# A two-layer encoder trunk on one core: the first modulation staged by channel block, and one product of each `down` parted at column 264

## The chip, the cores and the metric

The kernel runs on one core of a Trainium2 chip. The metric is the device time of one execution in microseconds (us), as the median of several runs. The core has a matrix engine (TensorE; PE in the profile, with its weight loads as PEld), a vector engine (VectorE, DVE), a scalar engine (ScalarE, ACT), GpSimd (POOL), and SyncE (SP), which here only issues DMAs.

## The reference

One batch of 256 tokens with 1024 channels goes through two layers. Each layer has three sub-layers, each with a modulated RMSNorm ahead of it and a gated residual behind it. All shifts, scales and gates come from the condition `c` by a matrix of 1024 x 9216 per layer.

```python
c_act = silu(c)
h = x
for l in range(2):
    mod = c_act @ ada_w[l] + ada_b[l]
    sh1, sc1, g1, sh2, sc2, g2, sh3, sc3, g3 = split(mod, 9)
    n1 = rms_norm(h, norm_g[l, 0]) * (1 + sc1) + sh1
    h = h + 0.5 * g1 * swiglu(n1, ffn_wg[l, 0], ffn_wu[l, 0], ffn_wd[l, 0])
    n2 = rms_norm(h, norm_g[l, 1]) * (1 + sc2) + sh2
    h = h + g2 * token_mixing(n2, ...)      # two kinds of attention, merged by gates
    n3 = rms_norm(h, norm_g[l, 2]) * (1 + sc3) + sh3
    h = h + 0.5 * g3 * swiglu(n3, ffn_wg[l, 1], ffn_wu[l, 1], ffn_wd[l, 1])
return rms_norm(h, final_g)
# swiglu(x, wg, wu, wd) = (silu(x @ wg) * (x @ wu)) @ wd, with d_ff = 2816
```

## The kernel before, in words

**Products of float32 in three parts.** Every float32 operand `r` is held as a rounded part `hi` (type fp32r) and a rest `lo = r - hi`. A product is `hi.hi + lo.hi + hi.lo`, three products of TensorE with one sum in PSUM (`mm3`, lines 85 to 87). For the weights ScalarE makes `whi` (a cast, line 307) and VectorE `wlo` (a subtraction, line 308); for the activations they are `nh` and `nl`, and `hh` and `hl` within an FFN.

**The stream of weights.** All weights and the ada matrix come from HBM in units of 1 MB (128 partitions x 2048 columns) in one fixed order, the list `stream`. `load_next` issues the DMAs of the next unit on SP into one of four `raw` buffers; `pump(n)` takes `n` half units: a half of a weight unit goes through `whi` and `wlo` into two of 23 slots, a half of an ada unit through a reduction over the partition's 1024 columns (`ada_col`, line 240: shift and scale of one block of 128 channels) or a multiply-add (`ada_gate`, line 256). A `raw` buffer is filled again when both halves are taken, and a slot is free when the last product with it has ended (`done`).

**An FFN.** d_ff is cut into 11 slabs of 256. `gate_up_mm` makes one slab: 8 channel blocks x 2 halves x (gate, up) x 3 = 96 products of 256 columns (the tokens), weights stationary. `gate_up_act` makes `hT = silu(g) * u` as `hh` and `hl`. `down(idx)` adds slab idx into four PSUM banks (two token halves t x two column halves hf): 24 products of 512 columns, `hT` stationary and the weights moving. The loop makes gate/up of slab idx and then `down(idx - 1)`; the last three `down` stand apart in the boundary with the residual and the next norm. `gate_bcast` adds the gate's vector over the partitions by four products with a matrix of ones (`gb`, lines 281 and 282) and is called at idx 7.

**The start.** The first sub-layer has no sub-layer ahead to hide behind. `c` is spread over the partitions (`cb`), both token halves are normed with one power operation on POOL each, scaled, transposed on TensorE (`nt`) and copied to `xsT`. `first` then goes through the eight channel blocks in four pairs u: `mod_k(u)` reduces two units of ada (scale and shift of two blocks), makes `nh` on ScalarE (line 1164), `nf` and `nl` on VectorE (lines 1165, 1167); `go(sl, u)` runs the products of the pair for each of four slabs at once (line 1180), so that eight PSUM banks are filled together. The weights of those four slabs come in units named `side`. Then `down(0)` follows, and the three other slabs' `down`.

**What sets the order.** The program is written in this order; a scheduler of the framework places the instructions of each engine, and `follow`, `queue` and `behind` add order without a wait. Each engine takes its instructions strictly in order.

Of the kernel before, what the change touches and what calls it, by code (L numbers as in the profile page):

```python
# [19 lines left out]
P = 128  # L20
# [16 lines left out]
CAP0, CAP1, CAP2, CAP3 = 12, 12, 14, 14  # L37

# [3 lines left out]
def trunk(tc, a):  # L42
    nc = tc.nc
    with (
# [69 lines left out]
        for hf in range(2):  # L114
            x = slice(hf * 512, (hf + 1) * 512)
            bank = gen("cb")
            nc.tensor.matmul(bank, ones[0:1, :], crow[hf], start=True, stop=True)
            cact = nc.scalar.activation(cb[:, x], bank, AF.Silu)
# [44 lines left out]
        for l, s in SUBS:  # L163
            w = weights(l, s)
            ad = list(ada_in[(l, s)])
            if (l, s) == (0, 0):
                c = cols(0, 0)
# [32 lines left out]
        def load_next():  # L200
            if nload[0] < len(stream):
# [3 lines left out]
                if u[0] == "side":  # L205

                    _, j, pr = u
                    for i in range(2):
                        x = slice((j % 2) * 1024, (j % 2 + 1) * 1024)
                        nc.sync.dma_start(raw[:, i * 1024:(i + 1) * 1024], a["w_gu"][0, 0, 2 * pr + i, j // 2][:, x])  # L210
# [24 lines left out]
        def ada_col(u, r, i):  # L235
# [6 lines left out]
            if i == 1:  # L242
# [3 lines left out]
                else:  # L246
                    tmp = small("sc1", (P, 2))
                    nc.vector.tensor_tensor(tmp, col[:, k], abc[:, l, s, 1, k], op=ALU.add)
                    nc.vector.scalar_tensor_tensor(m["a"][:, k], tmp, 1.0, ngc[:, l, s, k], op0=ALU.add, op1=ALU.mult)

# [42 lines left out]
        halves = {}  # L293
        pos = [0, 0]

        def pump(n=1):
            while n > 0 and pos[0] < len(stream):
                u = stream[pos[0]]
                isw = u[0] not in ("col", "gate")
# [4 lines left out]
                if isw:  # L304
                    hi = slot("whi", (P, 1024), F32R, "w")
                    lo = slot("wlo", (P, 1024), F32R, "w")
                    queue("act", nc.scalar.copy(hi, r))  # L307
                    queue("dve", nc.vector.tensor_tensor(lo, r, hi.bitcast(F32), op=ALU.subtract))  # L308
                    if u[0] == "side":
                        _, j, pr = u  # L310
                        halves[("gu", 0, 0, 2 * pr + i, j // 2, j % 2)] = (hi, lo)
                    else:
                        halves[u + (i,)] = (hi, lo)
# [226 lines left out]
        def ffn(i, nT, norm1, first, nT_next):  # L540
# [6 lines left out]
            def down_mm(idx, t, hf, last, y=slice(0, 512)):  # L547
# [602 lines left out]
        def first(nT, hT, down):  # L1150
# [4 lines left out]
            def mod_k(u):  # L1155
                pump(4)

                pump(1)
                m = mods[(0, 0)]
                nf = b2("nf", (P, 2, S))  # L1160
                for i in range(2):
                    k = 2 * u + i
                    src = xsT[k // 4][:, k % 4, :]
                    nc.scalar.activation(nh[:, k, :], src, AF.Identity, bias=m["sh"][:, k:k + 1], scale=m["a"][:, k:k + 1])
                    nc.vector.tensor_scalar(nf[:, i, :], src, m["a"][:, k:k + 1], m["sh"][:, k:k + 1], op0=ALU.mult, op1=ALU.add)
                kk = slice(2 * u, 2 * u + 2)
                behind["dve"] = nc.vector.tensor_tensor(nl[:, kk, :], nf, nh[:, kk, :].bitcast(F32), op=ALU.subtract)

            def go(sl, u):
                g, ub = banks[sl]  # L1170
                un, i = ("gu", 0, 0, sl, u // 2), u % 2
                wh, wl = half(un, i)

                for x, y in ((0, 0), (1, 0), (0, 1)):
# [10 lines left out]
            for u in range(4):  # L1185
                mod_k(u)
                if u % 2 == 1:
                    free(1)
# [119 lines left out]
```

## Time and profile before

| | |
|---|---|
| median of 3 runs | 1107.83 us (1107.62 to 1108.61) |
| profiled execution, device time | 1109.12 us |
| its span, first to last instruction | 1107.3 us |
| TensorE busy | 1089.7 us, 98% of the span, 7758 products |
| VectorE busy | 865.4 us, 78% |
| ScalarE busy | 588.7 us, 53% |
| POOL busy | 44.2 us, 4% |
| moved by DMA | 271.12 MB, mean 245 GB/s |

How to read it: the profile is one execution, some 1.8 us longer than the span of its instructions. "Busy" of TensorE runs from a product's start to its modelled end, so consecutive products overlap in it, and a busy TensorE can still take its products at different paces: the pace is the distance between the starts of two products. In a row of the timeline the first number is the start in us from the span's beginning, the second the duration in us.

### The profile page before, as it was taken

The numbers are of one execution on the slowest core, as the hardware profiler recorded it, in microseconds if no ns is written. First come the engines' busy times: TensorE is split into PE (matmuls) and PEld (weight loads), VectorE is DVE, ScalarE is ACT, GpSimd is POOL, SyncE is SP. The second block draws the span as 40 slices with busy tenths as digits, with TensorE's granted clock in tenths as the row PEclk, the third lists the DMA queues.
The fourth block names the chain that finished last, engine by engine and source line by source line (L and its number), as shares of the span: only waits on it lengthen the run. The fifth ranks groups of instructions, "written<-read, shape, count | busy, mean of one in ns | idle before, by whom it ended". The sixth has DMA issues, their size and how long they took to land.

```text
span 1107.3 us, 19106 instructions
## 1 busy us (share of the span) xinstructions
PE 1089.7 (98%) x7758; PEld 1008.1 (91%) x7758; DVE 865.4 (78%) x1378; ACT 588.7 (53%) x910; POOL 44.2 (4%) x52
## 2 busy tenths in 40 slices
PE   6999999999999999999999999999999999999997
PEld 5989999898999899999989999989889988999996
DVE  6997986899978798886589886469988779765543
ACT  5454473558664653535365445445776547544432
POOL 1000000230010000000000000004000000000000
PEclk9999999999999999999999999999999999999999
DMA  8998996379745298897449977553865455866501
GB/s 326 395 343 319 355 345 226 116 263 320 263 178 191 97 374 342 333 357 288 148 152 362 356 284 270 194 177 117 297 233 190 156 188 193 315 252 229 198 12 39
DMA packets 42585, 271.12 MB, mean 245 GB/s; under 512 B 5624, under 2 KB 6392, under 8 KB 12544
## 3 DMA queue, kind: packets, MB, share of 16 engines
q1 hardware_dynamic: 40036, 267.93, 65.6%
q10 hardware_dynamic: 2460, 1.96, 0.6%
q8 instruction: 61, 1.00, 0.3%
q14 instruction: 28, 0.23, 0.1%
HBM read 268.82 MB, written 1.05 MB: 244 GB/s over the span
## 4 chain that ended last, share of the span: by engine, by line
PE 90%; DVE 5%; ACT 2%; DMA 1%; issue 1%; POOL 0%; POOLq 0%; SPq 0%
PE dn L87 7%; PE dn L86 7%; PE dn L85 7%; PE g L85 6%; PE u L85 6%; PE g L87 6%; PE u L87 6%; PE g L86 6%; PE u L86 6%; PE g L1180 2%; PE u L1180 2%; PE gt L85 2%; PE gt L87 2%; PE gt L86 2%; PE yb L87 1%; PE yb L86 1%
## 5 line engine op out<-in xcount | busy, mean ns | idle before, releaser
L308 DVE TENSOR_TENSOR wlo<-raw,whi 128x1024 fp32r<-128x1024 f32 x364 | 437.2, 1222 | 136.2 <-PE u L86 86.1
L307 ACT CAST whi<-raw 128x1024 fp32r<-128x1024 f32 x364 | 373.3, 1051 | 219.0 <-PE u L87 83.1
L85 PE MATMUL g<-nh,whi 128*128 128x256 f32 x592 | 166.2, 281 | 0.0
L85 PE MATMUL u<-nh,whi 128*128 128x256 f32 x592 | 166.0, 280 | 0.0
L87 PE MATMUL g<-nl,whi 128*128 128x256 f32 x592 | 165.9, 280 | 0.0
L86 PE MATMUL g<-nh,wlo 128*128 128x256 f32 x592 | 165.9, 280 | 0.0
L87 PE MATMUL u<-nl,whi 128*128 128x256 f32 x592 | 165.9, 280 | 0.0
L86 PE MATMUL u<-nh,wlo 128*128 128x256 f32 x592 | 165.9, 280 | 0.0
L85 PE MATMUL dn<-whi,hh 128*128 128x512 f32 (+1 forms) x358 | 138.3, 386 | 0.0
L86 PE MATMUL dn<-whi,hl 128*128 128x512 f32 (+1 forms) x358 | 138.1, 386 | 0.0
L87 PE MATMUL dn<-wlo,hh 128*128 128x512 f32 (+1 forms) x358 | 138.1, 386 | 0.0
L240 DVE CUSTOM_DVE_ANT_0 raw<-raw,cb 128x1024 f32<-128x1024 f32 x96 | 114.7, 1219 | 3.3 <-DMA raw<-in_ada_t_dram 3.2
L87 PEld LDWEIGHTS u<-nl,whi 128*128 128x128 f32 x592 | 113.0, 191 | 0.1
L87 PEld LDWEIGHTS g<-nl,whi 128*128 128x128 f32 x592 | 113.1, 191 | 0.0
L86 PEld LDWEIGHTS g<-nh,wlo 128*128 128x128 f32 x592 | 111.3, 188 | 1.3
L85 PEld LDWEIGHTS g<-nh,whi 128*128 128x128 f32 x592 | 111.1, 188 | 1.4
L86 PEld LDWEIGHTS u<-nh,wlo 128*128 128x128 f32 x592 | 111.3, 188 | 0.0
L85 PEld LDWEIGHTS u<-nh,whi 128*128 128x128 f32 x592 | 111.1, 188 | 0.0
L87 PEld LDWEIGHTS dn<-wlo,hh 128*128 128x128 f32 x358 | 67.2, 188 | 13.6
L86 PEld LDWEIGHTS dn<-whi,hl 128*128 128x128 f32 x358 | 67.3, 188 | 12.3
L85 PEld LDWEIGHTS dn<-whi,hh 128*128 128x128 f32 x358 | 67.3, 188 | 12.3
L521 ACT ACTIVATE sg<-g 128x512 f32<-128x512 f32 x41 | 24.5, 597 | 95.6 <-PE g L87 94.4
(209 smaller groups left out, 2018.1 us busy)
## 6 DMA issues: line engine op xcount, KB each, us to landing
raw<-in_w_gu_dram SPq DMA_DIRECT2D x79, 1024.0 KB, 5.0
raw<-in_w_d_dram SPq DMA_DIRECT2D x41, 1024.0 KB, 6.3
raw<-in_ada_t_dram SPq DMA_DIRECT2D x40, 1024.0 KB, 6.2
raw<-in_ada_g_dram SPq DMA_DIRECT2D x24, 1024.0 KB, 6.6
raw<-in_w_in_dram SPq DMA_DIRECT2D x16, 1024.0 KB, 4.8
raw<-in_w_gate_dram SPq DMA_DIRECT2D x16, 1024.0 KB, 4.9
raw<-in_w_gu_dram SPq DMA_DIRECT2D x18, 512.0 KB, 7.0
raw<-in_ada_t_dram SPq DMA_DIRECT2D x16, 512.0 KB, 7.3
```

The costliest lines, as they stand in the source:

```text
L85: nc.tensor.matmul(out, Lh, Rh, start=start, stop=False, skip_group_check=True)
L86: nc.tensor.matmul(out, Ll, Rh, start=False, stop=False, skip_group_check=True)
L87: nc.tensor.matmul(out, Lh, Rl, start=False, stop=stop, skip_group_check=True)
L240: queue("dve", nc.vector.tensor_tensor_reduce(r, r, cb, 1.0, 0.0, op0=ALU.mult, op1=ALU.add, accum_out=col[:, k:k + 1]))
L307: queue("act", nc.scalar.copy(hi, r))
L308: queue("dve", nc.vector.tensor_tensor(lo, r, hi.bitcast(F32), op=ALU.subtract))
L521: nc.scalar.activation(sg, g, AF.Silu)
L1180: nc.tensor.matmul(bank[:, c * 256:(c + 1) * 256], W[:, w], N[:, k, :], start=x + y + k + c == 0, stop=y == 1 and k == NK - 1, skip_group_ ...
```

## The change

1. **Stages of one block.** In the stream the first ada units and the first four slabs come as `colk` k (scale and shift of block k, 1 MB) and `side` k (block k of four slabs, 1 MB, four DMAs of 256 KB), for k = 0 to 7. `first` goes through eight blocks instead of four pairs; `nf` is made on ScalarE like `nh`; products of a stage go over all four slabs with `nh.whi`, then `nh.wlo`, then `nl.whi`; in the last stage by pairs of slabs, each with all three, so that the first two slabs' activations start earlier.
2. **The norm by halves.** The sums of squares of both token halves go through one power operation of two columns, with a small one ahead of it on POOL that nothing waits for. Channels 0 to 511 of both halves are scaled on ScalarE, transposed and copied first; channels 512 to 1023 are scaled on VectorE (`tail_scale`) behind the first block's modulation.
3. **Identity products.** `keep_busy` runs products of the identity with itself, 512 columns of float32, whose result nothing reads: two behind `cb`, one behind the last transposes.
4. **Down products parted.** In `down` (not in the boundary's last three slabs) the very last product of the 24, `hh.wlo` for t = 1, hf = 1, c = 1, is done as two, columns 0 to 263 and 264 to 511 of the bank.
5. **Gate broadcast earlier.** At idx 7 `gate_bcast` is called ahead of `down(6)` instead of behind it.

```diff
+PART = 264
...
-                for j in range(4):
-                    stream += [c.pop(0), c.pop(0)]
-                    stream += [("side", j, p) for p in range(SIDE // 2)]
+                for k in range(NK):
+                    stream += [("colk", k), ("side", k)]
...
+        def ada_colk(k, r, i):
+            m = mod_of(0, 0)
+            which = 1 - i
+            col = m["raw"][which]
+            queue("dve", nc.vector.tensor_tensor_reduce(r, r, cb, 1.0, 0.0, op0=ALU.mult, op1=ALU.add,
+                                                        accum_out=col[:, k:k + 1]))
+            x = slice(k, k + 1)
+            if which == 0:
+                m["last"] = nc.vector.tensor_tensor(m["sh"][:, x], col[:, x], abc[:, 0, 0, 0, x], op=ALU.add)
...
-            def down_mm(idx, t, hf, last, y=slice(0, 512)):
+            def down_mm(idx, t, hf, last, y=slice(0, 512), part=False):
...
                 for c in range(2):
                     x = slice(c * 512 + y.start, c * 512 + y.stop)
+                    if part and c == 1:
+
+                        for L, R in ((hh, wh), (hl, wh)):
+                            nc.tensor.matmul(acc[t][hf], L[:, c, tok], R[:, x], start=False, stop=False, skip_group_check=True)
+                        for z in (slice(0, PART), slice(PART, 512)):
+                            nc.tensor.matmul(acc[t][hf][:, z], hh[:, c, tok], wl[:, 512 + z.start:512 + z.stop], start=False,
+                                             stop=idx == NS - 1, skip_group_check=True)
+                        continue
...
-                    down_mm(idx, 1, hf, 2)
+                    down_mm(idx, 1, hf, 2, part=hf == 1)
...
                 hT[idx] = gate_up_act(g, u)
+                if idx == 7:
+                    gate_bcast(l, s)
...
-                if idx == 7:
-                    gate_bcast(l, s)
-                    if s == 0:
-                        consts = mixer_consts(l, consts)
+                if idx == 7 and s == 0:
+                    consts = mixer_consts(l, consts)
...
+            for k in range(NK):
+                pump(2)
...
+                if k == 0:
+                    in_turn("act", modulate(nh[:, k, :]))
                     pump(1)
+                    behind["act"] = copies(1, behind["act"])
+                    nfi = modulate(nf)
+                    pump(1)
+                    queue("act", nfi)
+                else:
+                    behind["dve"] = m["last"]
+                    pump(2)
+                    behind["act"] = split[1]
+                    in_turn("act", modulate(nh[:, k, :]))
+                    in_turn("act", modulate(nf))
+                behind["dve"] = split[0]
+                in_turn("dve", nc.vector.tensor_tensor(nl[:, k, :], nf, nh[:, k, :].bitcast(F32), op=ALU.subtract))
+                if k < NK - 1:
+                    for x, y in ((0, 0), (1, 0), (0, 1)):
+                        for p in range(2):
+                            go(k, p, x, y)
...
+        keep_busy(gen("busy"), 2, cmm)
+
+        pow_half(small("pw", (P, 1)), ones[:, 0:1])
...
+        rstd = small("rstd", (P, 2))
+        pow_half(rstd, ms)
...
+        def tail_scale():
+
+            for t in range(2):
+                xs = b2("xs")
+                ins = nc.vector.tensor_scalar(xs, h[t][:, 512:1024], rstd[:, t:t + 1], None, op0=ALU.mult)
+                follow(ins, m0["last"])
+                tr = turn(1, t, xs)
+            keep_busy(accb("busy"), 1, tr)
+            return ins
```

What this makes of the order shows at three places. The first is VectorE in the first stages; `raw ... cb` is a reduction of ada, `sc`, `ma` and `msh` are the small operations of scale and shift. Before, the second pair of blocks, from its third reduction on:

```order
L240 ISA raw_195,mraw_180<-raw_195,cb 128x1024
L240 ISA mraw_180 128x1
L248 TENSOR_TENSOR sc_60_324<-mraw_181,abc 128x2
L240 ISA raw_195,mraw_180<-raw_195,cb 128x1024
L240 ISA mraw_180 128x1
L249 SCALAR_TENSOR_TENSOR ma_182<-sc_60_324,ngc 128x2
L308 TENSOR_TENSOR wlo_337<-raw_236,whi_336 128x1024
L245 TENSOR_TENSOR msh_183<-mraw_180,abc 128x2
L308 TENSOR_TENSOR wlo_341<-raw_236,whi_340 128x1024
L1165 TENSOR_SCALAR nf_347<-xsT_117,ma_182,msh_183 128x256 x2
L1167 TENSOR_TENSOR nl_116<-nf_347,nh_115 128x512
```

And with the change, the whole second block:

```order
L260 ISA raw_108,mraw_160<-raw_108,cb 128x1024
L260 ISA mraw_160 128x1
L260 ISA raw_108,mraw_159<-raw_108,cb 128x1024
L260 ISA mraw_159 128x1
L268 TENSOR_TENSOR sc_55_267<-mraw_160,abc 128x1
L269 SCALAR_TENSOR_TENSOR ma_161<-sc_55_267,ngc 128x1
L264 TENSOR_TENSOR msh_162<-mraw_159,abc 128x1
L330 TENSOR_TENSOR wlo_277<-raw_111,whi_276 128x1024
L330 TENSOR_TENSOR wlo_281<-raw_111,whi_280 128x1024
L1229 TENSOR_TENSOR nl_120<-nf_275,nh_119 128x256
```

A block now has two reductions, two `wlo` and one `nl`, each in the place of four, four and one larger for a pair, and no `nf`. The second place is TensorE between a `down` and the next gate/up series. Before, the end of `down(2)`:

```order
L85 MATMUL dn_797<-whi_760,hh_753 128x512
L86 MATMUL dn_797<-whi_760,hl_754 128x512
L87 MATMUL dn_797<-wlo_761,hh_753 128x512
L85 MATMUL g_925<-nh_115,whi_790 128x256
L86 MATMUL g_925<-nh_115,wlo_791 128x256
```

With the change:

```order
L578 MATMUL dn_851<-whi_797,hh_837 128x512
L578 MATMUL dn_851<-whi_797,hl_838 128x512
L580 MATMUL dn_851<-wlo_798,hh_837 128x264
L580 MATMUL dn_851<-wlo_798,hh_837 128x248
L86 MATMUL g_986<-nh_119,whi_827 128x256
L87 MATMUL g_986<-nh_119,wlo_828 128x256
```

The last product ahead of the series has 248 columns where it had 512. The third place is TensorE at the start, with the change (before, no `busy` row stands there, and all 16 transposes come one after the other):

```order
L118 MATMUL cb_92<-crow_72,ones_88 128x512
L118 MATMUL cb_95<-crow_73,ones_88 128x512
L1264 MATMUL busy_123<-ident 128x512 x2
L1290 MATMUL nt_145<-ident,xs_143 128x128 x4
L1290 MATMUL nt_152<-ident,xs_150 128x128 x4
L1290 MATMUL nt_185<-ident,xs_183 128x128 x4
L1290 MATMUL nt_192<-ident,xs_190 128x128 x4
L1264 MATMUL busy_197<-ident 128x512
L1199 MATMUL g_34_166<-nh_119,whi_201 128x256
```

The third and fourth group of transposes and the last identity product stand ahead of the first gate/up product.

## Rows read from the trace of the kernel before

**Rows 1.** The page, part 1: busy us (share of the span) x instructions.

```profile
PE 1089.7 (98%) x7758; PEld 1008.1 (91%) x7758; DVE 865.4 (78%) x1378; ACT 588.7 (53%) x910; POOL 44.2 (4%) x52
```

**Rows 2.** The page, part 5: operation, count | busy us, mean ns | idle before, its releaser.

```profile
L308 DVE TENSOR_TENSOR wlo<-raw,whi 128x1024 fp32r<-128x1024 f32 x364 | 437.2, 1222 | 136.2 <-PE u L86 86.1
...
L521 ACT ACTIVATE sg<-g 128x512 f32<-128x512 f32 x41 | 24.5, 597 | 95.6 <-PE g L87 94.4
```

**Rows 3.** Timeline of TensorE, from `down` to gate/up: start us, duration us, operation.

```profile
129.60 0.39 PE L87 MATMUL dn<-wlo,hh 128*128 128x512 f32 x1
129.83 0.28 PE L85 MATMUL g<-nh,whi 128*128 128x256 f32 x1
129.94 0.28 PE L86 MATMUL g<-nh,wlo 128*128 128x256 f32 x1
```

**Rows 4.** Windows over the 26 slow stretches, TensorE: length, busy (products), clock, DMA.

```profile
1061.05:1083.67 22.62, 22.62 (x194) 1.00 0.00 1
sum 327.86, PE 327.86; mean PE 12.61
```

**Rows 5.** Windows of 8 us in other series, the last within `yb`.

```profile
150.00:158.00 8.00, 8.00 (x73) 1.00 0.86 308
585.00:593.00 8.00, 8.00 (x73) 1.00 1.02 382
...
328.00:336.00 8.00, 8.00 (x69) 1.00 0.48 176
```

**Rows 6.** Timeline of TensorE, end of the first stage and first `down`.

```profile
62.57 0.28 PE L1180 MATMUL g<-nl,whi 128*128 128x256 f32 x1
...
63.25 0.39 PE L85 MATMUL dn<-whi,hh 128*128 128x512 f32 x1
...
63.95 0.39 PE L85 MATMUL dn<-whi,hh 128*128 128x512 f32 x1
```

**Rows 7.** Timeline of TensorE, what stands ahead of other series.

```profile
147.04 0.39 PE L281 MATMUL gb<-gh,onesr 128*128 128x512 f32 x1
...
276.29 0.93 PE L846 MATMUL pt<-ident,p 128*128 128x128 f32 x7
...
277.17 0.28 PE L86 MATMUL gt<-nh,wlo 128*128 128x256 f32 x1
277.29 0.28 PE L87 MATMUL gt<-nl,whi 128*128 128x256 f32 x1
...
583.85 0.60 PE L533 MATMUL tb<-ident,ht 128*128 128x128 f32 x4
```

**Rows 8.** Timeline of TensorE at the start.

```profile
2.40 3.77 PE L117 MATMUL cb<-crow,ones 1*128 1x512 f32 x4 [2.40 <-POOL ones L111]
...
16.84 0.58 PE L1180 MATMUL g<-nh,whi 128*128 128x256 f32 x1 [1.29 <-ACT nh L1164]
...
22.77 0.30 PE L1180 MATMUL u<-nh,whi 128*128 128x256 f32 x1
```

**Rows 9.** Timeline of VectorE, from the second pair's first `wlo` to the third's.

```profile
27.48 1.23 DVE L308 TENSOR_TENSOR wlo<-raw,whi 128x1024 fp32r<-128x1024 f32 x1
...
38.51 0.74 DVE L1165 TENSOR_SCALAR nf<-xsT,ma,msh 128x256 f32<-128x256 f32 x2
39.16 1.22 DVE L308 TENSOR_TENSOR wlo<-raw,whi 128x1024 fp32r<-128x1024 f32 x1
```

**Rows 10.** Timeline of POOL, VectorE and ScalarE at the start.

```profile
8.65 0.55 POOL L123 TENSOR_TENSOR rstd<-ms,mhalf 128x1 f32<-128x1 f32 x1 [6.31 <-DVE ms L359]
9.14 1.23 DVE L240 CUSTOM_DVE_ANT_0 raw<-raw,cb 128x1024 f32<-128x1024 f32 x1 [0.64 <-DMA raw<-in_ada_t_dram]
9.23 1.34 ACT L370 ACTIVATE xs<-h,rstd 128x512 f32<-128x512 f32 x2 [1.21 <-POOL rstd L123]
...
14.73 1.07 ACT L307 CAST whi<-raw 128x1024 fp32r<-128x1024 f32 x1
...
16.16 1.11 ACT L1164 ACTIVATE nh<-xsT,msh,ma 128x256 fp32r<-128x256 f32 x2
```

More of the change, by code (lines that the diff above doesn't have):

```diff
@@ L116, in trunk @@
             bank = gen("cb")
-            nc.tensor.matmul(bank, ones[0:1, :], crow[hf], start=True, stop=True)
+            cmm = nc.tensor.matmul(bank, ones[0:1, :], crow[hf], start=True, stop=True)
             cact = nc.scalar.activation(cb[:, x], bank, AF.Silu)
@@ L298, in pump @@
                 u = stream[pos[0]]
-                isw = u[0] not in ("col", "gate")
+                isw = u[0] not in ("col", "colk", "gate")
                 if isw and live["w"] + 2 > min(cap_w[0], NSLOT - live["a"]):
@@ L1185, in first, with in_turn, go @@
[L1185 to L1188, printed above, removed]
-                for sl in range(SIDE):
-                    go(sl, u)
-                    pump(1)
-                    if u == 3:
+            m = mod_of(0, 0)
+            def in_turn(eng, ins):
+                queue(eng, ins)
+                behind[eng] = ins
+                return ins
+            def go(k, p, x, y):
+                W, N = halves[("side", k, p)][x], (nh, nl)[y]
+                for e in range(2):
+                    for c in range(2):
+                        for j, bank in enumerate(banks[2 * p + e]):
+                            w = slice(e * 512 + j * 256 + c * P, e * 512 + j * 256 + (c + 1) * P)
+                            nc.tensor.matmul(bank[:, c * 256:(c + 1) * 256], W[:, w], N[:, k, :],
+                                             start=x + y + k + c == 0, stop=y == 1 and k == NK - 1, skip_group_check=True)
@@ new lines, in first, with modulate @@
+            for k in range(NK):
+                pump(2)
+                behind.clear()
+                if k == 0:
+                    behind["dve"], behind["act"] = m["last"], copied[0]
+                    in_turn("dve", tail_scale())
+                src = xsT[k // 4][:, k % 4, :]
+                col = slice(k, k + 1)
+                nf = b2("nf", (P, S))
+                def modulate(dst):
+                    return nc.scalar.activation(dst, src, AF.Identity, bias=m["sh"][:, col], scale=m["a"][:, col])
+                if k == 0:
+                    in_turn("act", modulate(nh[:, k, :]))
+                    pump(1)
+                    behind["act"] = copies(1, behind["act"])
+                    nfi = modulate(nf)
+                    pump(1)
+                    queue("act", nfi)
+                else:
+                    behind["dve"] = m["last"]
[9 more added lines that the diff above has]
+                            go(k, p, x, y)
+                    for p in range(2):
+                        done(("side", k), p, 0)
+                    if k % 4 == 3:
+                        free(1)
+                    continue
+                behind.clear()
+                for p in range(2):
+                    for x, y in ((0, 0), (1, 0), (0, 1)):
+                        go(k, p, x, y)
+                    done(("side", k), p, 0)
+                    pump(2)
+                    for sl in (2 * p, 2 * p + 1):
@@ L1195, in first @@
                         hT[sl] = gate_up_act(*banks[sl])
-                        pump(1)
+                        pump(2)
+                free(1)
         for _ in range(RAW_BUFS):
@@ L1204, in trunk, with keep_busy @@
         xsT = [slot("xsT", (P, 4, S)) for _ in range(2)]
+        ident4 = ident.rearrange("p (r x) -> p r x", r=1).broadcast_to([P, 4, P])
+        def keep_busy(bank, n, first_):
+            for _ in range(n):
+                ins = nc.tensor.matmul(bank.rearrange("p (r x) -> p r x", r=4), ident, ident4, start=True, stop=True)
+                follow(ins, first_)
+                first_ = ins
+        keep_busy(gen("busy"), 2, cmm)
+        pow_half(small("pw", (P, 1)), ones[:, 0:1])
         ns = [Norm(t) for t in range(2)]
```

84 lines of the change are left out of this document (42 added, 42 removed).

## The prediction

> **What bounds the kernel now.** I read the page's busy shares first, then its costliest groups, then the timeline of TensorE by single products, then busy time by windows. TensorE is busy 98% of 1107.3 us [rows 1]. The largest group on VectorE, the `wlo` subtractions, stands idle mostly until a product has ended [rows 2]: the supplier waits for TensorE to free a buffer. So outside the first 60 us a microsecond off TensorE's own sequence is a microsecond off the span; an earlier weight is worth nothing.
>
> The timeline shows that this sequence is not uniform. In the gate/up loop a product of 256 columns starts every 113 or every 118 ns. After a clean run of `down` products (512 columns, 227 ns apart) the gate/up products come about 118 ns apart [rows 3] and stay so to the end of the series. I found 26 such stretches: the first begins at 79.59 us, the last at 1061.05. Their windows sum to 327.86 us [rows 4]; by the loops they hold 20 x 96 + 4 x 192 + 72 + 24 = 2784 products, so 117.8 ns each. Other stretches of the same loop run quicker: a window of 8 us touches 73 products, and 69 where `yb` is computed [rows 5]; at 117.8 ns it touches 8000 / 117.8 + 2 = 70. The quick pace is six products from 62.57 to 63.25, 113.3 ns [rows 6]. A series keeps the pace it begins with, until something else stands between its products. What stands before it decides:
> - after `down` at its steady 227 ns: slow in 25 of 25 series;
> - after a gate broadcast (`gb`), whose products come 235 ns apart, mostly quick: the `gb` product at 147.04 us is followed by a quick series [rows 5, 7]; of five series behind such products four are quick within four products, one stays slow;
> - after transposes of 128 columns: quick behind `tb` at 583.85 [rows 5, 7], slow (0.12 us) behind `pt` at 276.29 [rows 7]; in the whole trace 17 quick, 9 slow.
>
> The second place is the start. The first gate/up product starts at 16.84 us; TensorE's products are at the lower of its two clock levels, 1.2 GHz, until 22.77 us, 5.93 us after steady work began [rows 8]. 27 products took that time; at 113.3 ns they would take 3.06, so 2.9 us are lost there.
>
> **1. The parted product: what it can do to the series behind it.** The change parts the last product of each of the first eight `down` calls of an FFN, 32 in all, into 264 and 248 columns over the same weights. 27 of them stand directly ahead of a gate/up series, 26 of these slow now. The trace shows no product of 248 columns, so its effect is bounded by the nearest rows: nothing (the series stay at 117.8), the quick pace of 113.3, or the worst pace shown, 69 in 8 us, about 120 ns [rows 5]. I take the quick pace. The slow pace follows only where every product before had 512 columns and an undisturbed 227 ns spacing; anything shorter or later before a series ends in the quick pace more often than not (17 of 26, 4 of 5), and a 248-column product is shorter than the 256 behind it, so that the next weights are not yet in when it ends. And since `down` always settles at 227 ns, all 27 places look alike to the engine: I expect all to flip, or none. 2784 x (117.8 - 113.3 ns) = **-12.4 us**; ends 0 and +6.2 (at 120 ns).
>
> **2. What it costs.** Behind a quick series the first three `down` products take 0.70 us (63.25 to 63.95) [rows 6] against 3 x 227 = 0.68: 27 times some 0.015, **+0.4**. The pair itself has 512 columns as before; between 0 and 13 ns more (two products at 120), 32 times, **+0.2**, ends 0 and 0.4.
> The Trainium skill, "TensorE: Matmul & The Clock Gate", section "Back-to-back issue gap", gives N / 2.4 ns plus a fixed 2.5 ns per product, whatever stands before it. By that rule parting only adds 32 x 2.5 ns, under 0.1 us, and nothing else changes. The rows disagree: the same 256 columns take 113, 118 or 120 ns, none of them the rule's 109.2; it is a rival below.
>
> **3. The gate broadcast moved ahead of `down`.** Its products, in the first FFN and the last, now stand inside `down(6)`, the first behind four `down` products (0.91 us after gate/up 7 ends). Its operand `gh` comes after the `silu` on ScalarE, 0.60 us [rows 2], and takes about as long: some 1.2 us, so up to 0.3 us of waiting, perhaps once more for `gl`. **+0.2**, ends 0 and 1.
>
> **4. The start, first product.** DVE's first reduction starts at 9.14 us when its half has landed [rows 10]; the DMAs ahead of it are the same, so this stays. Two reductions (1.22 us each) and three small operations instead of four and three: the modulation of block 0 is ready at about 12.1. Beside it the norm: the power op began at 8.65 and took 0.55 [rows 10]; with both tiles' sums ahead and two columns I take 8.8 to 9.5, then two `xs` in 1.34 [rows 10], transposes and two copies to 12.3. `nh` takes half of 1.11, `whi` 1.07 [rows 10]: 14.0. Ahead of the first product TensorE now also holds eight transposes fed by DVE's `tail_scale` (to 13.4) and an identity product: 14.8 at the full clock, 16.1 at the lower one. For the clock: the `cb` products fill 2.40 to 6.17 [rows 8], two identity products of the same width and type follow at once, as long again, together 7.5 us of steady work against the 5.93 after which the clock rose. So I take the full clock, 14.8.
>
> **5. The start, the pace.** In a stage of one block DVE does two reductions, two `wlo`, one `nl` of 256 columns, three small operations; TensorE 48 products, 5.44 us at 113.3 ns. Before, a pair of blocks took DVE from 27.48 to 39.16, 5.84 per block, with a `nf` of 0.37 per block in it [rows 9], which goes to ScalarE (idle about half the time). That leaves 5.5; the small operations come once a block instead of once a pair, 0.1. I take 5.6, so DVE sets the pace, not TensorE; ends 5.44 (TensorE) and 5.84 (nothing saved). Block 0 is slower: `whi` of the second pair stands behind two copies and `nf` on ScalarE, ready at 16.7, its `wlo` at 17.9, `nl` at 18.3. Seven blocks later 18.3 + 39.2 = 57.5. TensorE then has 32 products left, 3.6 us: 61.1. `down(0)` must also wait for hT[0], which is behind three `wlo` (3.5 us) and two shorter operations (0.6 each) on DVE: 62.2, less the one product that needs only `hh`: 61.9. `down` started at 63.25 before [rows 6]: **-1.4**, ends -2.5 (5.44 per block) and +0.5 (5.84, with a late power op). What is late next is DVE. The slow clock, if it stays, lies mostly beside DVE's lag in block 0 and is inside these ends. After 63 us DVE has its lead: its `wlo` wait for TensorE more than for anything else, 86.1 of 136.2 us [rows 2], so a TensorE that is 1% faster does not run dry.
>
> **Sum.** -12.4 + 0.4 + 0.2 + 0.2 - 1.4 = -13.0 us. The profiled execution took 1109.12: 1096.1. The median of the runs is 1107.83, 1.3 below it: **1094.8 us**. With the ends of the terms the forecast's own range is 1092.8 to 1097.0. What a measurement of this kernel can tell from no change is about 0.2%, 2.2 us.
>
> **Rivals.**
> - *Half of it* (0.09): the pair's effect depends on the phase in which `down` ended, and a series is slow again in every second place: -6.2 for -12.4, about 1101. Or the first stage is slower, 6.5 us a block, with TensorE waiting in each: +6, the same time. For it: one of the five series behind `gb` stayed slow. Against it: `down` has one steady spacing.
> - *The parting does nothing for the series behind it* (0.13): the pace belongs to operands and buffers. Only the start is left, -1.4 + 0.2 + 0.2: 1106.8. For it: 9 of 26 series behind short products are slow. By the rule of the Trainium skill named above it would end here too.
> - *The parting sets the worst pace* (0.06): `yb` always runs at 69 in 8 us [rows 5], also directly behind 512-column products. If the pair puts the 27 series at 120 ns, 2784 x 2.2 = +6.1 us, and 192 quick ones lose 1.3 more; with the start and the costs, 1107.83 + 6.1 + 1.3 + 0.8 - 1.4 = 1114.6. It decides from 118.5 ns a product on, where 2784 x 0.7 ns outweighs the start. Against it: no gate/up series of the trace ran at it.
>
> **How the numbers follow.** The forecast has 0.72. The range takes in its own ends and the half case: 1092.8 to 1101, 0.81. Faster by over 0.2%: forecast and half case, and a small part of the third where the start gives its full -2.5: 0.82. Within 0.2%: the rest of that rival, 0.12. Slower: 0.06.
>
> **What would show it.** Right: in windows of 8 us inside the gate/up loop 73 products instead of 70, from the third `down` on; `down` series that begin with about 232 ns; the first stage ending near 62 us with VectorE busy throughout and TensorE waiting for `nl` or `nh`; products at 113 ns from the first. Wrong: 70 in 8 us behind the pairs (then the parting does nothing, whatever the start gives), 69 or fewer (worst pace), or waits of TensorE for `wlo` after 63 us.

## The result, and the profile after

The changed kernel takes **1097.44 us** (median of 4 runs, 1097.19 to 1098.11) against 1107.96 us before in the same session: ratio 0.9903, 95% interval 0.989 to 0.9915. Its profiled execution took 1097.68 us, 11.4 below the 1109.12 of the one before. 1094.8 was forecast, with a range of 1092.8 to 1101.0.

The page, parts 1 and 5, of the changed kernel, with the columns of [rows 1, 2]:

```profile
PE 1082.9 (99%) x7796; PEld 998.8 (91%) x7796; DVE 864.9 (79%) x1388; ACT 593.1 (54%) x916; POOL 44.5 (4%) x52
...
L330 DVE TENSOR_TENSOR wlo<-raw,whi 128x1024 fp32r<-128x1024 f32 x364 | 436.9, 1220 | 133.7 <-PE u L87 44.6
```

TensorE has 38 products more and is busy 6.8 us less; VectorE hardly changed (864.9 against 865.4 us). The difference lies in the pace of the same products. The timeline of TensorE at the end of `down(2)`, the place of [rows 3]:

```profile
127.59 0.40 PE L580 MATMUL dn<-wlo,hh 128*128 128x264 f32 x2
127.83 0.28 PE L86 MATMUL g<-nh,whi 128*128 128x256 f32 x1
127.94 0.28 PE L87 MATMUL g<-nh,wlo 128*128 128x256 f32 x1
128.06 0.28 PE L88 MATMUL g<-nl,whi 128*128 128x256 f32 x1
128.18 0.28 PE L86 MATMUL u<-nh,whi 128*128 128x256 f32 x1
128.30 0.28 PE L87 MATMUL u<-nh,wlo 128*128 128x256 f32 x1
128.42 0.28 PE L88 MATMUL u<-nl,whi 128*128 128x256 f32 x1
128.53 0.28 PE L86 MATMUL g<-nh,whi 128*128 128x256 f32 x1
128.65 0.28 PE L87 MATMUL g<-nh,wlo 128*128 128x256 f32 x1
128.76 0.28 PE L88 MATMUL g<-nl,whi 128*128 128x256 f32 x1
128.87 0.28 PE L86 MATMUL u<-nh,whi 128*128 128x256 f32 x1
```

The first five distances are about 118 ns as before, then 113. Two windows of 8 us behind pairs, and at the foot the sum of the 27 windows from each pair's end to the next product that is not gate/up (the length; busy time and instructions of PE, PEld, DVE, ACT and POOL; clock, DMA share, GB/s):

```profile
80.00:88.00 8.00, 8.00 (x73) 8.00 (x72) 7.77 (x7) 2.00 (x2) 0.00 (x0) 1.00 0.99 380
...
1052.00:1060.00 8.00, 8.00 (x73) 8.00 (x73) 3.67 (x3) 2.11 (x2) 0.00 (x0) 1.00 0.00 0
...
sum 317.64, PE 317.52 PEld 317.32 DVE 207.26 ACT 120.28 POOL 0.00; mean PE 11.76 PEld 11.75 DVE 7.68 ACT 4.45 POOL 0.00
```

By the loops these windows hold 2794 products: 317.64 / 2794 = 113.7 ns, where [rows 4] gave 117.8. All 27 series behind a pair are quick.

The start gave less than was forecast. POOL, VectorE, ScalarE and TensorE there, then TensorE at the end of the first stages:

```profile
8.60 1.62 POOL L124 TENSOR_TENSOR rstd<-ms,mhalf 128x2 f32<-128x2 f32 x1 [5.61 <-DVE ms L1282]
8.44 1.22 DVE L260 CUSTOM_DVE_ANT_0 raw<-raw,cb 128x1024 f32<-128x1024 f32 x1
10.25 1.33 ACT L1303 ACTIVATE xs<-h,rstd 128x512 f32<-128x512 f32 x2 [2.22 <-POOL rstd L124]
11.03 3.67 PE L1290 MATMUL nt<-ident,xs 128*128 128x128 f32 x16 [1.13 <-ACT xs L1303]
15.39 0.68 PE L1199 MATMUL g<-nh,whi 128*128 128x256 f32 x1
...
62.18 0.40 PE L86 MATMUL dn<-whi,hh 128*128 128x512 f32 x1
```

The first gate/up product came at 15.39 instead of 14.8 us, the first `down` at 62.18 instead of 61.9. Before it was 63.25 [rows 6], so 1.1 us are won, of which 0.9 is left where the first loop series starts (78.73 against 79.59).

### The profile page after: what moved, and what is told of

Same layout as the page of the kernel before. It is cut to its first block, busy times and chain, and to the rows that moved or that the text cites. A ratio compares the mean times of both kernels' runs of the same rounds, so it can differ in the third digit from the quotient of the medians.

```text
span 1095.9 us, 19235 instructions
## 1 busy us (share of the span) xinstructions
PE 1082.9 (99%) x7796; PEld 998.8 (91%) x7796; DVE 864.9 (79%) x1388; ACT 593.1 (54%) x916; POOL 44.5 (4%) x52
## 4 chain that ended last, share of the span: by engine, by line
PE 94%; DVE 3%; ACT 1%; issue 1%; POOL 0%; POOLq 0%
PE dn L87 6%; PE dn L88 6%; PE dn L86 6%; PE u L86 6%; PE g L86 6%; PE u L87 6%; PE g L88 6%; PE g L87 6%; PE u L88 6%; PE gt L86 3%; PE gt L88 3%; PE gt L87 3%; PE g L1199 2%; PE u L1199 2%; PE yb L88 1%; PE yb L87 1%
## 5 line engine op out<-in xcount | busy, mean ns | idle before, releaser
L87 PE MATMUL u<-nh,wlo 128*128 128x256 f32 x592 | 163.7, 277 | 0.0
L88 PE MATMUL u<-nl,whi 128*128 128x256 f32 x592 | 163.6, 276 | 0.0
L86 PE MATMUL dn<-whi,hh 128*128 128x512 f32 (+1 forms) x326 | 126.0, 387 | 0.0
L87 PE MATMUL dn<-whi,hl 128*128 128x512 f32 (+1 forms) x326 | 125.9, 386 | 0.0
L88 PE MATMUL dn<-wlo,hh 128*128 128x512 f32 (+1 forms) x326 | 125.8, 386 | 0.0
L245 DVE CUSTOM_DVE_ANT_0 raw<-raw,cb 128x1024 f32<-128x1024 f32 x80 | 95.5, 1217 | 1.1 <-DMA raw<-in_ada_t_dram 0.9
L86 PE MATMUL gt<-nh,whi 128*128 128x256 f32 x256 | 73.7, 288 | 0.0
L88 PEld LDWEIGHTS dn<-wlo,hh 128*128 128x128 f32 x326 | 61.2, 188 | 12.4
L87 PEld LDWEIGHTS dn<-whi,hl 128*128 128x128 f32 x326 | 61.3, 188 | 11.1 <-DVE hl L546 0.2
L86 PEld LDWEIGHTS dn<-whi,hh 128*128 128x128 f32 x326 | 61.3, 188 | 11.1
```

The costliest lines, as they stand in the source:

```text
L86: nc.tensor.matmul(out, Lh, Rh, start=start, stop=False, skip_group_check=True)
L87: nc.tensor.matmul(out, Ll, Rh, start=False, stop=False, skip_group_check=True)
L88: nc.tensor.matmul(out, Lh, Rl, start=False, stop=stop, skip_group_check=True)
L245: queue("dve", nc.vector.tensor_tensor_reduce(r, r, cb, 1.0, 0.0, op0=ALU.mult, op1=ALU.add, accum_out=col[:, k:k + 1]))
```

## The experiments

Each kernel ran beside runs of the kernel before on the same chip, whose medians went from 1108.66 to 1109.07 us (1107.96 beside the changed kernel); so ratios are what compares.

**The pair alone taken away.** `down_mm(idx, 1, hf, 2, part=hf == 1)` becomes `down_mm(idx, 1, hf, 2)`.

> The changed kernel with the last product of each down whole again; all else of the change stays. My theory (the pair alone turns the 26 series behind it from 117.8 to 113.3 ns a product, and the rest of the change is worth about 1 us): 1107.3 us, 9.5 to 10.5 above the changed kernel, with 70 products in a window of 8 us behind each down and 118 ns between them. Rival (the new order of the start and of the stream, not the pair, sets the rhythm of what follows): at most 3 us above the changed kernel, 1097.5 to 1100.5, with 113 ns kept in most series.

Measured: 1107.81 us, ratio 0.9993 (0.9984 to 1.0002). The windows behind `down` are back at 70:

```profile
80.00:88.00 8.00, 8.00 (x70) 8.00 (x70) 6.21 (x6) 2.01 (x2) 0.00 (x0) 1.00 0.99 389
```

So with the new start in place the pair is worth 0.0090 of the time, 10.0 us, and the rest of the change by itself nothing that can be measured. The rival falls.

**The pair alone added to the kernel before.** The `part` branch of the diff and `PART = 264`, nothing else.

> The kernel before with the parting at 264 alone; start, stages, norm and gate broadcast as before. My theory: 1097.6 to 1098.6 us, about 9.8 below the kernel before, the 26 slow series all at 113.6 ns on average, the first down still starting near 63.2 us. Rival (the pair works only together with the new start): above 1104.

Measured: 1105.13 us, ratio 0.9967 (0.9955 to 0.998), only 3.6 us. That is the rival's number without its reason: the series are all quick, and yet some 6 us are missing. In the profiled execution they are lost in one place. TensorE's rows around the first FFN's gate broadcast, with what it waited for in brackets, and three windows of 4 us:

```profile
145.03 0.40 PE L282 MATMUL gb<-gh,onesr 128*128 128x512 f32 x1
145.67 0.49 PE L86 MATMUL dn<-whi,hh 128*128 128x512 f32 x1 [0.24 <-ACT whi L308]
148.76 0.79 PE L283 MATMUL gb<-gl,onesr 128*128 128x512 f32 x1 [2.60 <-DVE gl L281]
```

```profile
144.00:148.00 4.00, 1.92 (x9) 1.13 (x7) 4.00 (x8) 3.04 (x4) 0.00 (x0) 0.97 1.01 365
148.00:152.00 4.00, 3.24 (x12) 2.95 (x13) 4.00 (x8) 1.53 (x2) 0.95 (x1) 0.50 0.99 408
152.00:156.00 4.00, 4.00 (x25) 3.90 (x25) 2.76 (x4) 3.19 (x4) 0.00 (x0) 0.67 0.77 271
```

TensorE, now quicker, waits for `gl`, was busy 1.92 us of 4, and then works at the lower level, 1.2 GHz (granted clock 0.50), with 213 ns between two products of 256 columns until 154.5 us. The series of slabs 9 and 10 starts at 168.42 us here and at 163.96 before: 4.5 us lost by then, 9 won behind it (last series at 1056.48 against 1061.05). In the changed kernel no such wait stands there: TensorE is busy 11.88 of the 12 us from 140 to 152, at full clock.

Why is `gl` late? Two things show on VectorE, which is busy for all of 144 to 152 us. Its first `gl` starts at 148.02 us, behind a `wlo`, two reductions of ada and `hl`; in the kernel before (142.28 us) and in the changed kernel (139.83) it stands directly behind the slab's multiplication `sg`. And 40 us earlier VectorE had stood idle for two small loads, constants of the token mixing:

```profile
104.25 0.17 DVE L682 TENSOR_SCALAR bg<-bg 128x16 f32<-128x16 f32 x1 [3.33 <-DMA bg<-in_b_gate_col_dram]
106.80 0.15 DVE L683 TENSOR_SCALAR subg<-subg 128x1 f32<-128x1 f32 x1 [2.37 <-DMA subg<-in_subln_col_dram]
```

In the kernel before and in the changed one it waits there for the first of them alone (2.86 and 2.77 us). No run moved these loads, so how much of the 6 us is theirs stays open.

**Where the cut lies.** `PART = 248` and `PART = 384`.

> The changed kernel with the cut at column 248 instead of 264, so that the last product of a down has 264 columns, more than the 256 behind it. The reason that my prediction gave (the last product is shorter than the 256 columns behind it, so the next weights are not yet in when it ends) says: nothing flips, about 1107.5 us, 118 ns a product. Rival (any break in the even 227 ns spacing of the 512-column products flips the series, whatever its length): 1097.4, as with 264.

> The changed kernel with the cut at column 384, the last product has 128 columns. Both my reason and its rival (any break) say that all series stay quick; the pair costs more, because a 128-column product of this type comes no closer than some 112 ns (the od products of the trace) where its columns alone would be half of a 256-column one's 113: 170 + 112 ns against 232, so 32 x 0.05 = 1.6 us: 1099.0 us. A third view (the phase that 264 + 248 happens to leave is what counts): series behind it mixed or slow, 1102 or more.

Measured: with 248 1108.71 us, ratio 1.0001 (0.9992 to 1.001); with 384 1098.53, 0.9909 (0.9896 to 0.9923). With 248 the pair costs the same 0.23 us, but 26 of the 27 series behind it stay slow; with 384 all 27 are quick. TensorE's timeline at the start of slab 3 of the second FFN, cut at 248, and a window of its last series:

```profile
416.79 0.40 PE L580 MATMUL dn<-wlo,hh 128*128 128x248 f32 x2
417.02 0.28 PE L86 MATMUL g<-nh,whi 128*128 128x256 f32 x1
...
417.97 0.28 PE L88 MATMUL g<-nl,whi 128*128 128x256 f32 x1
418.08 0.28 PE L86 MATMUL u<-nh,whi 128*128 128x256 f32 x1
```

```profile
1062.00:1070.00 8.00, 8.00 (x70) 8.00 (x70) 3.68 (x3) 2.11 (x2) 0.00 (x0) 1.00 0.00 0
```

Nine distances in 1.06 us: 118 ns to the end. Of three cuts the two whose last product is shorter than the 256 columns behind it turn every series; behind the longer one a single series is quick, the ten products from 145.31 to 146.33 us (113 ns apart). They stand behind `down(6)` of the first FFN, among whose products the gate broadcast now lies; at the same place of the last FFN the series is slow. So "any break in the rhythm" is refuted, and so is a phase that only 264 happens to leave.

The reason given for it, that the next weights are not yet in, does not show in the records of the weight loads. First the changed kernel (the product itself starts at 127.83 us), then the cut at 248 (417.02 us):

```profile
127.72 0.19 PEld L86 LDWEIGHTS g<-nh,whi 128*128 128x128 f32 x1
...
416.90 0.19 PEld L86 LDWEIGHTS g<-nh,whi 128*128 128x128 f32 x1
```

Each load starts with the last product of `down`, takes 0.19 us, and by the record ends 0.07 to 0.08 us after the first gate/up product has started, in the quick case as in the slow one. Why the shorter last product sets the quicker pace stays open.

**Is it the broadcast's place, or VectorE as a whole?** First the kernel before with the pair and with the first FFN's `gate_bcast` at index 5, ahead of `down(4)`:

```diff
+                if idx == 5 and i == 0:
+                    gate_bcast(l, s)
                 if idx == 1:
...
                 if idx == 7:
-                    gate_bcast(l, s)
+                    if i > 0:
+                        gate_bcast(l, s)
```

> The parting alone on top of the kernel before, as in the run that came out at 1105 instead of 1098, but with the first FFN's gate broadcast called ahead of down(4) at index 5, where its operand gl has no reductions of ada ahead of it on VectorE. My theory (what the parting alone lost is one wait: TensorE stood for gl from 145 to 149 us, because the scheduler had put gl behind two reductions, and its clock was at the lower level until about 154 us after it; some 6 us in all): the wait and the low clock are gone, 1098.0 to 1099.5 us. Rival (VectorE as a whole is too late in the first FFN for a quicker TensorE, as long as nf stays with it): TensorE waits elsewhere before 170 us, for a wlo or an hl, 1101.5 or more.

Measured: median 1103.27 us, but executions from 1099.41 to 1106.14; ratio 0.9956 (0.9938 to 0.9973). The profiled one, among the best with 1100.13, shows the wait at the new place too:

```profile
112.30 0.40 PE L282 MATMUL gb<-gh,onesr 128*128 128x512 f32 x1
114.35 0.50 PE L283 MATMUL gb<-gl,onesr 128*128 128x512 f32 x1 [1.66 <-DVE gl L281]
115.02 0.50 PE L283 MATMUL gb<-gl,onesr 128*128 128x512 f32 x1
```

This is the rival's number, with a wait for `gl` instead of a `wlo` or `hl`. Here `gl` stands directly behind `sg`, so the order was not all of it; VectorE had again stood for the two small loads, 0.58 and 2.01 us ahead of 101.35 and 103.53 us. Next, `nf` of the first stages made on ScalarE in that kernel (line 1165: `nc.scalar.activation` with bias and scale, as for `nh`). The recorded text says 16 `nf`; there are eight, 3 us in all.

> The kernel before with the parting, with the gate broadcast at index 5 and with nf made on ScalarE, as in the changed kernel; pairs of blocks, norm and weight order stay as before. Without nf's move this kernel's executions went from 1099.4 to 1106.1 us, median 1103.3. My theory (in the first FFN VectorE is the bound once TensorE is quicker; its 16 nf, 16 x 0.37 = 5.9 us... of which 3 us are left as lead at 63 us, decide whether TensorE waits): 1097.5 to 1099.5 us and executions within 1.5 us of each other. Rival (it is not VectorE's lead but the new stages' order of the weights that keeps TensorE fed): still a median above 1101 with a spread of some us.

Measured: 1101.59 us, 1100.21 to 1102.44; ratio 0.9929 (0.9917 to 0.9942): neither forecast. The spread is 2.2 us (five executions) instead of 6.7 (seven), and the wait for `gl` 0.6 instead of 1.66 us. This does not show that VectorE's load decides, though. VectorE began `gl` later than without the move (114.77 against 113.61 us), and TensorE came later still: in pairs of blocks `nf` on ScalarE delays `nh`, TensorE waits 3.1 us for it instead of 1.8, and the first `down` starts at 65.26 instead of 63.02.

What goes with the wait in the profiles is the load of `subg`. VectorE stood for it at 100 to 107 us with the pair alone (2.37 us), in these two runs (2.01 and 1.58) and in one below (1.39), and these are the runs in which TensorE waited over 0.5 us for `gl` of the first FFN (2.60, 1.66, 0.56, 0.68). In no other run with the broadcast at these places did it stand for `subg`. That is one profile of each run and no test: whether `nf`, the stages, the order of VectorE or the arrival of these loads is the new start's cure stays open.

**The other parts of the change.** The gate broadcast behind `down(6)` again:

> The changed kernel with the gate broadcast behind down(6) again, as before. The order of VectorE is the same as with it ahead (gl behind the same instructions). My theory (VectorE sets when gl is there, and it is there in time): within 0.8 us of the changed kernel, 1096.8 to 1098.2. Rival (the earlier call is what keeps TensorE from waiting for gl at 145 us): a wait of 2 us or more and the lower clock behind it, 1101 or more.

Measured: 1096.99 us, ratio 0.9893 (0.9878 to 0.9908), as the theory has it: no difference from the changed kernel can be measured. The identity products taken out (both calls of `keep_busy`):

> The changed kernel without the three identity products. In four runs with them TensorE's clock was up at the transposes from 11 us in two and only at 15 to 16 us in the other two, so they help in some executions only. My theory (the low clock lies beside VectorE's and ScalarE's lag in the first block, where TensorE waits for nh for 0.9 us anyway): the first gate/up products at 213 ns until about 16.5 us, first down 0 to 0.4 us later, time within 0.5 us of the changed kernel, 1097.0 to 1097.9. Rival (the identity products carry the gain of the start): first down after 63 us, 1098.5 or more.

Measured: 1097.77 us, ratio 0.9894 (0.9879 to 0.9909); first `down` at 62.47: no difference either.

**The start's two surprises.** A small operation holds the first reduction back behind the power operation:

```diff
+        rtail = small("rtail", (P, 2))
+        behind["dve"] = nc.vector.tensor_scalar(rtail, rstd, 1.0, None, op0=ALU.mult)
...
-                ins = nc.vector.tensor_scalar(xs, h[t][:, 512:1024], rstd[:, t:t + 1], None, op0=ALU.mult)
+                ins = nc.vector.tensor_scalar(xs, h[t][:, 512:1024], rtail[:, t:t + 1], None, op0=ALU.mult)
```

> The changed kernel with the first reduction of ada held back until the power operation on POOL is done (a small operation on VectorE that reads its result stands ahead of it). In the changed kernel that operation took 1.62 us beside a running reduction of VectorE; before it took 0.55 us while VectorE was idle, and 1.46 us beside one. My theory (POOL is slow while VectorE runs its reduction): the power operation takes 0.5 to 0.8 us, the first xs starts near 9.5 instead of 10.25, the first gate/up product up to 0.7 us earlier; the time 0 to 0.7 lower, 1096.7 to 1097.4. Rival (two columns cost that much by themselves): still 1.6 us, everything of the start 0.7 later, 1097.5 to 1098.2.

Measured: 1096.96 us, ratio 0.989 (0.9875 to 0.9904); POOL and ScalarE:

```profile
8.88 0.71 POOL L124 TENSOR_TENSOR rstd<-ms,mhalf 128x2 f32<-128x2 f32 x1 [5.89 <-DVE ms L1282]
9.63 1.33 ACT L1305 ACTIVATE xs<-h,rstd 128x512 f32<-128x512 f32 x2 [1.59 <-POOL rstd L124]
```

0.71 us with VectorE idle, against 1.62 beside its reduction: the theory on POOL holds, two columns are not the reason. The first gate/up product gains nothing, it stands at 15.55. `xs` is 0.6 us earlier, but the reductions and `tail_scale` behind them are 1.3 later (12.33 us instead of 11.06), TensorE stands 1.19 us for its result, and then makes the last eight transposes at the lower level (granted clock 0.50 from 12.90 to 14.50 us; 1.97 us against 1.27 for the first eight). The time lies in the theory's range, and it is not told from the changed kernel's.

**More places to part.** Every stage's last product and the first one of `yb`, at 128 columns each; then, without `yb`, the stages, the held reduction and an order that keeps the weights' parts behind the slabs' activations (`behind["act"]` and `behind["dve"]` set to the two instructions of `gate_up_act` ahead of `pump(2)`):

```diff
+                            cuts = (0, 128, 256) if y == 1 and p + e + c + j == 4 and k < NK - 1 else (0, 256)
+                            for z0, z1 in zip(cuts, cuts[1:]):
+                                nc.tensor.matmul(bank[:, c * 256 + z0:c * 256 + z1], W[:, w], N[:, k, z0:z1],
```

> The changed kernel, with two more places parted: the last product of each of the eight first stages into 128 + 128 columns, and the first product of each yb call into 128 + 128. In the changed kernel seven of the eight stages ran at 118 ns a product, and yb at 120. My theory (a short product ahead of a series lets it run at 113 ns if nothing waits in it): stages at 113 ns, the first down at 60.8 instead of 62.2 us, -1.2; yb, 4 x 96 products, from 120 to 113.5: -2.5 less 4 x 0.06. Together 1094.0 us. Rival for yb (its pace comes from its operands, one step of 24 products has the same pattern 117, 121, 120, 124 from its first products on): yb stays at 120, and 1096.3 in all. Rival for the stages (VectorE or the weights' arrival holds them): the first down stays after 61.8.

> The changed kernel with three edits: the first reduction held behind the power operation, the last product of each of the first seven stages in 128 + 128 columns, and the weights' parts taken behind the first slabs' activations on ScalarE and VectorE, so that the quicker stages are not lost to the order as when yb was parted too. My theory: all stages at 113 ns, first down near 60.8 us (62.2 in the changed kernel), no wait of over 0.6 us behind it, 1095.6 us, 1095.0 to 1096.4. Rival (VectorE then is what is late: TensorE waits as long as it gained): first down or a wait before 64 us that eats it, 1096.9 to 1097.8.

Measured: 1100.87 us, ratio 0.9923 (0.9909 to 0.9938), and 1097.99, 0.9896 (0.9883 to 0.991). Neither time met a forecast. The stages' products come 113 ns apart where nothing waits (73 in 8 us from 40 to 48), but the stages gain little: from the first product to the first of the eighth stage it is 40.7 and 41.2 us (14.62 to 55.32, 14.29 to 55.50), against 41.1 in the changed kernel (15.39 to 56.52). In the first run TensorE then stands 1.48 us for `hh`, because the scheduler had put four `wlo` ahead of the slabs' multiplications on VectorE, and `down` starts at 62.53. Its profiled execution, 1099.10, is the quickest of four, so the trace does not show where the median's other 2 us went. `yb` does not follow at all:

```profile
326.00:334.00 8.00, 8.00 (x69) 8.00 (x69) 5.00 (x8) 3.28 (x5) 0.00 (x0) 1.00 0.40 139
```

69 in 8 us, as in [rows 5]: behind its 128-column products it is back at 120 ns after some ten products. In the second, `down` starts at 61.01, since the first product was 1.1 us earlier. Half of this lead is lost at 143 us, where TensorE waits 0.7 us for `gl`, and the rest before the first `yb`. So the broadcast was put at index 8, and one more product parted, the last of the token-major gate/up (512 columns, ahead of the series of 85):

> The run before this one (stages parted, power operation alone, 0.9896 of the kernel before) lost 0.7 us of its lead at 143 us, where TensorE waited 1.07 us for gl on VectorE. Two edits on it: the gate broadcast at index 8 instead of 7, where VectorE has caught up, and the last product of each FFN's token-major gate/up (512 columns, directly ahead of a series of 85 that is slow in some executions) parted at 264. My theory: no wait for gl over 0.4 us, TensorE's gate/up of slab 9 starts at 160.6 instead of 161.7 us, the three series of 85 quick (0.4 us each where they were slow); 1.0 to 1.8 us in all, a ratio of 0.9882 +- 0.0008. Rival (what comes behind is held by VectorE or the DMAs in the mixer and gives it back): slab 9 earlier, but the first yb still at 324.1 us, ratio 0.9890 to 0.9898.

Measured: 1098.51 us, ratio 0.9906 (0.9889 to 0.9922), no better and outside both forecasts. The first `down` starts at 60.37, and TensorE then waits for `gh` on ScalarE:

```profile
157.92 0.39 PE L88 MATMUL dn<-wlo,hh 128*128 128x512 f32 x1
160.02 0.50 PE L301 MATMUL gb<-gh,onesr 128*128 128x512 f32 x1 [1.71 <-ACT gh L299]
```

The first `yb` starts at 324.06 us, as in the changed kernel (324.10) and the run before (324.08): the rival's sign, but what gives the lead back was not looked for. The new pair turned none of its three series (383.52, 568.25, 919.12), which are slow behind 248 columns; the third was quick in the changed kernel (918.91).

```profile
383.52 0.28 PE L88 MATMUL u<-nl,whi 128*128 128x256 f32 x1
...
383.99 0.28 PE L86 MATMUL u<-nh,whi 128*128 128x256 f32 x1
```

Four distances in 0.47 us. No version was measurably better than the changed kernel.

## Why the prediction was right, and where not

1. **The pair (forecast -12.4 us): right in size; its reason holds at this place only, and how it works stays open.** 2784 products went from 117.8 to 113.7 ns, -11.4. Most of the missing 1.0 us is the entry: the term took 113.3 ns from the first product on, but each series begins with five distances of 116 to 123 ns, 26 ns more than at 113.3, which is 0.7 us over 27 series. Another 0.3 us is a wait inside one of the windows (146.19 to 146.59, ahead of a `gb` product).

   The condition given, a last product shorter than the 256 columns behind it, is what the three cuts bear out behind `down`. It is no general rule: 264 + 248 ahead of the series of 85 turned none of three, and 248 + 264 let one of 27 be quick. The prediction's other wording, "anything shorter or later ... more often than not", fails behind `down`, where 264 columns, shorter than 512, turned 1 of 27; and "the slow pace follows only" behind even products of 512 had 9 slow series of the prediction's own count against it. That the next weights are late was argued and does not show in the records.

   The rival that the parting does nothing is refuted. The prediction gave it a rule of the Trainium skill, "TensorE: Matmul & The Clock Gate", section "Back-to-back issue gap"; but that section gives it as the gap of an isolated product and says that in a stream of weight loads and products both set the spacing. As a price for this stream it does not serve: removing the pair cost 10 us, where that rule has under 0.1.
2. **Its cost (+0.6): right.** A `down` between two such series takes 5.46 us (89.63 to 95.09) instead of 5.44 (90.89 to 96.33), 0.02 each and some 0.5 for 27.
3. **The gate broadcast (+0.2): right.** From `down(6)` to slab 9 it is 23.42 us in the first FFN and 22.99 in the last, against 23.40 and 22.77 with the call moved back: 0.2, too little to show in the time.
4. **The start's first product (14.8 us): wrong, 15.39, and what failed is the clock.** The prediction took the full clock because of the identity products. `cb` and two of these worked from 2.41 to 9.89 us, yet the 16 transposes from 11.03 took 3.67 us, the lower level; so the 5.93 us of work ahead of the rise in [rows 8] was no measure for it. In three other runs the same instructions came out at full clock. One of them, the run without the pair, on TensorE:

```profile
10.91 2.14 PE L1290 MATMUL nt<-ident,xs 128*128 128x128 f32 x16 [1.02 <-ACT xs L1303]
...
14.42 0.39 PE L1199 MATMUL g<-nh,whi 128*128 128x256 f32 x1 [0.51 <-ACT whi L328]
```

   The others (the cut at 248, and the stages and `yb` parted) have 14.52 and 14.62: all earlier than the forecast. A second step was wrong, but these runs share it (1.62 us each), so it does not make the miss: the power operation was to end at 9.5 us and ended at 10.22. Its 0.7 us, from [rows 10] and two columns, is what it takes alone (0.71). But VectorE began its reduction at 8.44, without a pause, and beside that it took 1.62. The Trainium skill, "SBUF — State Buffer", section "SBUF: two separate sides", says that VectorE with two SBUF operands and POOL share one pair of ports and that the later one waits out the whole instruction. The trace agrees: the reduction ended at 9.66, and the operation 0.56 later.
5. **The pace of the stages (5.6 us, set by VectorE): the number right, the engine wrong.** VectorE's stages were 5.23 us apart (`nl` at 24.00, 29.23, 34.46). The 5.6 came from [rows 9] less one `nf` per block, but that stretch holds the `nf` of two pairs, those at 38.51 us and these:

```profile
29.82 0.74 DVE L1165 TENSOR_SCALAR nf<-xsT,ma,msh 128x256 f32<-128x256 f32 x2
```

   So 0.74 us per block went, not 0.37: 5.84 - 0.74 + 0.1 = 5.2. TensorE took 5.65, since its series of 48 fell into the slow pace behind the first wait, where the text had 5.44 for it:

```profile
28.00:36.00 8.00, 8.00 (x70) 8.00 (x69) 7.97 (x16) 3.78 (x6) 0.00 (x0) 1.00 1.03 379
```

   In other runs of the same stages some were quick (73 in 8 us from 36 to 52 us with the cut at 248, first `down` at 60.66). VectorE was priced too high and TensorE too low, so 5.6 against 5.65 is luck.
6. **"A TensorE that is 1% faster does not run dry": the premise on which the terms were added, and it did not hold for each alone.** It is true of the changed kernel and false of the kernel before with the pair. The sum has -11.8 for the pair with its costs and -1.4 for the start. By themselves they measure -3.6 and -0.8 (not told from nothing); together -10.5. About 6 us of the pair's worth hang on the rest of the change, with which `gl` is there when TensorE comes; by which part of it is not shown. The sum came out near because both were made at once. Of its 13.0 us it lacks 1.6 in the profiled execution (11.4): 1.0 in part 1, 0.5 at the start (78.73 us, -0.9 for -1.4), and 0.1 that is not put down to anything.

## What to carry to other kernels

Where a long series of equal products runs a few per cent over its best pace, look at what stands directly ahead of it: shortening that one product below the length of those that follow bought 1% here, but try it at each kind of place, since two others did not answer. And before adding up two gains, ask whether the engine that becomes quicker finds its suppliers early enough without the other one: here the first bought a third of its worth alone. Where a supplier is late, look back on it for an idle wait, even for a load of a few columns, before calling it overloaded. A duration from a row holds for what ran beside it there.

## What was not expected of the hardware

- Two lengths go with two lasting paces: 264 + 248 and 384 + 128 at the end of `down` give 113 ns a product in 27 of 27 series, 248 + 264 gives 118 in 26 of 27, and the pace lasts for 96 or 192 products.
- A wait of TensorE of about 3 us at 145 to 149 us was followed by a granted clock of 0.50 from 148 to 152 us and 0.67 from 152 to 156; at 213 instead of 113 ns a product that lost nearly 3 us more (an estimate from these rows).
- The same instructions at the start get the full clock before 11 us in some executions and only after 14 us in others. In the three with the early clock the second block starts at 21.68 to 21.88 us, against 22.50 in the changed kernel; they differ from it in other places too, so no run shows what this is worth in the total time.
- A power operation of POOL on 128 x 2 elements takes 0.71 us alone and 1.62 beside a reduction of VectorE.
